# Moving operands of 256 tokens kept as two rows of 128, at another place in each partition

## The chip, the cores and the metric

The kernel runs on one core of a Trainium2 chip. The metric is the device time of one execution in microseconds; a lower time is better. The figure of a kernel is the median of several executions.

## What is computed

A transformer block and a second one of another build, for one sequence of 256 tokens of width 1024, in float32. The first block adds a gated sum of two mixers (a stick-breaking attention and an RWKV-7 time mix, eight heads of 64 each) and a SwiGLU network of width 2816. The second adds a mixer of a dilated-window attention and a short gated convolution, an attention to 256 tokens of a memory, and a network of width 4096 with a squared ReLU. Nearly all the work lies in products of the 256 tokens with weight matrices:

```python
proj = h @ w_in[l]
merged = (gates[..., :D] * (o_sb @ w_sb_out[l]) + gates[..., D:] * (o_rw @ w_rw_out[l]))
x = x + rms_norm(merged @ w_o[l], norm_mix_post[l])
h = rms_norm(x, norm_ffn_pre[l])
f = (jax.nn.silu(h @ w_ffn_gate[l]) * (h @ w_ffn_up[l])) @ w_ffn_down[l]
...
x = x + hybrid_mixer(rms_norm_2(x, g_mix), w_in, conv_w, g_attn_out, g_conv_out, w_out)
x = x + memory_cross_attention(rms_norm_2(x, g_xattn), rms_norm_2(mem, g_mem), w_q_mem, w_kv_mem, w_o_mem)
x = x + squared_relu_mlp(rms_norm_2(x, g_mlp), w_up, w_down)
return rms_norm_2(x, g_final)
```

## The kernel before, in words

Activations lie with features on the 128 partitions and tokens along them: a tile of `KC` chunks of 128 features holds, in each partition, `KC` times 256 tokens of 4 bytes. A float32 product is made of three products in the faster format `F32R`: each operand is kept as a rounded part (`xh`, `whi`) and a remainder (`xl`, `wlo`), and `whi` with `xh`, `whi` with `xl` and `wlo` with `xh` are summed in PSUM.

Weights come in slabs of 512 KB (`slab`, L185): one transfer on SyncE's queue, a copy on ScalarE that rounds (`whi`, L193), a subtraction on VectorE (`wlo`, L194). Three slabs are fetched ahead, in the order that `plan` wrote down at the start. For each slab `block` (L242) issues 24 matmuls at L258: two groups of 128 output features, four chunks of the contraction, three products each. A weight of 128 x 128 is the stationary operand, the 256 tokens of one chunk are the moving one. With `tok=True` it is the other way round: tokens are stationary, and 256 columns of the weight slab move; eight groups are made so (two for the values of the first attention, two for those of the dilated one, four for the values of the memory). The last product, `tokens` (L216), moves 512 columns of weights past tokens that are stationary (`ah`, `al`), through the helper `mm` (L273).

Where a tile lies in its partition is set by the order and the size of the pools; `shift` (L119) puts an unused tile of so many bytes ahead, and writes one element of it on GpSimd. So `PHASE` bytes stand before `xh`, and further shifts before the pools `one`, `gap` and `mlp`. With them every tile whose tokens move (`xh`, `xl`, `zh`, `zl`, `gh`, `gl`, `fh`, `fl`, `memh`, `meml`, `yh`, `yl`, `xoh`, `xol`, `sh`, `sl`, `oh`, `ol`) begins 192 bytes past a multiple of 512, a chunk is 1,024 bytes in one run, and slabs begin at a multiple of 512.

Tiles of tokens are written by `split` (L275: a copy on ScalarE, a subtraction on VectorE), by `normed` through it, and by `scaled` (L320: the same pair for one chunk, with a factor). In `hybrid` the factors of the norm lie in tiles of its own pool (`rm`, `r2`); the attention's factor is `ra`, the convolution's `rs`, both in the pool `tmp` with one buffer each. In `first`, chains of small steps (the recurrence, the first attention) are woven between the groups of matmuls, a step at each slab.

Matmuls whose operands are plain float32 (`px`, `py`, the transposes `tr`) take their columns at half the rate; in `px<-R,TT` the 128 moving columns are two runs of 64, in `px<-y,TT` one run. VectorE's product into `kap` (L596) works on runs of 64.

Of the kernel before, what the change touches and what calls it, by code (L numbers as in the profile page):

```python
# [8 lines left out]
F32 = mybir.dt.float32  # L9
F32R = mybir.dt.float32r  # L10
# [22 lines left out]
PHASE = 192  # L33
# [58 lines left out]

class Net:
    def __init__(self, ctx, tc, io):
        self.tc, self.nc, self.io = tc, tc.nc, io
        self.last_table = None
        self.queue, self.ready = [], []
        self.t2 = 3
        self.side = None
        nc = self.nc  # L100
        pool = lambda name, bufs=1, **k: ctx.enter_context(tc.tile_pool(name=name, bufs=bufs, **k))
        self.keep = pool("keep")
        self.cst = self.keep.tile([P, NRES], F32, name="cst")
        self.vec = self.keep.tile([P, NVEC], F32, name="vec")
        self.small = self.keep.tile([P, 8], F32, name="small")
        self.ones = self.keep.tile([P, P], F32, name="ones")
        self.pr = pool("wraw", 3)
        self.ph = pool("whi", 4)
        self.pl = pool("wlo", 4)


        acts = pool("acts")
        self.shift(acts, PHASE)
        self.xh = acts.tile([P, KC, T], F32R, name="xh")
        self.xl = acts.tile([P, KC, T], F32R, name="xl")
        self.zh = acts.tile([P, NP, T], F32R, name="zh")
        self.zl = acts.tile([P, NP, T], F32R, name="zl")
# [124 lines left out]
    def block(self, ps, name, g, b, xh, xl, tok):  # L242
        per = blocks(name)
        hi, lo, k0, m = self.next_slab(name, g * per + b)
        if isinstance(xh, list):
            xh, xl = xh[b], xl[b]
        cols = width(name) // P
        for c in range(cols):
            cc = slice(c * P, (c + 1) * P)
            for k in range(m):  # L250
                for t, (w, a) in enumerate(((hi, xh), (hi, xl), (lo, xh))):
                    first = b == 0 and c == 0 and k == 0 and t == 0
                    last = b == per - 1 and c == cols - 1 and k == m - 1 and t == 2
                    if tok:
                        lhsT, rhs = a[:, k0 + k, cc], w[:, k, :]
                    else:
                        lhsT, rhs = w[:, k, cc], a[:, k0 + k, :]
                    self.nc.tensor.matmul(ps[:, c, :], lhsT, rhs, start=first, stop=last,  # L258
                                          skip_group_check=True)
# [15 lines left out]
    def split(self, src, hi, lo):  # L275

        self.nc.scalar.copy(hi, src)
        self.nc.vector.tensor_sub(lo, src, hi.bitcast(F32))
# [14 lines left out]
    def rstd_sum(self, pool, parts, width, tag, square=None):  # L293
# [5 lines left out]
        r = pool.tile([P, T], F32, tag=tag, name=tag)  # L299
# [20 lines left out]
    def scaled(self, src, gname, hi, lo, first=0):  # L320

        for i, s in enumerate(src, first):
            for j in range(2):
                k, g = 2 * i + j, self.v(gname, 2 * i + j)
                self.nc.scalar.activation(hi[:, k, :], s[:, j, :], AF.Copy, scale=g)
                self.nc.vector.scalar_tensor_tensor(lo[:, k, :], s[:, j, :], g, hi[:, k, :].bitcast(F32),  # L326
# [17 lines left out]
    def normed(self, pool, src, r, gname, hi, lo):  # L344

        for i, s in enumerate(src):
# [4 lines left out]
            self.split(h, hi[:, 2 * i:2 * i + 2, :], lo[:, 2 * i:2 * i + 2, :])  # L351
# [75 lines left out]
def first(n):  # L427
    nc, tc = n.nc, n.tc
    with ExitStack() as ctx:
# [25 lines left out]
        gh = xg.tile([P, KC, T], F32R, name="gh")  # L455
        gl = xg.tile([P, KC, T], F32R, name="gl")
# [319 lines left out]
        sh = b4.tile([P, NP, T], F32R, tag="b4", name="sh")  # L776
        sl = b4.tile([P, NP, T], F32R, tag="b4", name="sl")
# [28 lines left out]
        def sb_values(j):  # L806
# [8 lines left out]
            n.split(of, sh[:, j, :], sl[:, j, :])  # L815
# [154 lines left out]
        def normalized():  # L970
# [4 lines left out]
            oh, ol = norm["o"] = [s4.tile([P, NP, T], F32R, tag="s4", name=k) for k in ("oh", "ol")]  # L975
# [12 lines left out]
            for i in range(2):  # L988
# [10 lines left out]
                n.split(yi, oh[:, ii, :], ol[:, ii, :])  # L999
# [14 lines left out]
        for g in range(4):  # L1014
# [6 lines left out]
            n.split(t, hi[:, 2 * g:2 * g + 2, :], lo[:, 2 * g:2 * g + 2, :])  # L1021
# [30 lines left out]
def ffn(n, tmp, wide, filler):  # L1052
    nc, tc = n.nc, n.tc
    with tc.tile_pool(name="ffn", bufs=1, reuse_waits="tile") as pool:
# [5 lines left out]
        fh = pool.tile([P, FF // P, T], F32R, name="fh")  # L1060
        fl = pool.tile([P, FF // P, T], F32R, name="fl")
        for g in range(FF // 256):
# [8 lines left out]
            n.split(m, fh[:, 2 * g:2 * g + 2, :], fl[:, 2 * g:2 * g + 2, :])  # L1071
# [4 lines left out]
def memory(n, mem, wide, tmp, kT, vm):  # L1076
# [4 lines left out]
    mh = mem.tile([P, KC, T], F32R, name="memh")  # L1081
    ml = mem.tile([P, KC, T], F32R, name="meml")
# [21 lines left out]
def hybrid(n, tmp, kv):  # L1104
    nc, tc = n.nc, n.tc
    with ExitStack() as ctx:
        pool = ctx.enter_context(tc.tile_pool(name="hyb", bufs=1, reuse_waits="tile"))
        yh = pool.tile([P, KC, T], F32R, name="yh")
        yl = pool.tile([P, KC, T], F32R, name="yl")
        r2 = pool.tile([P, T], F32, name="r2")  # L1110
        rs = []

        def norms():
            acc = n.squares(tmp, pairs(n.x))
            rs.append(pair(n.rstd_sum(pool, [acc], D, "rm", r2)))
# [90 lines left out]
        def conv_norm():  # L1206
            rc = n.rstd(tmp, pairs(cv), 512, "rs")
            kv(4, n.ax("kv").rearrange("p (c t) -> p c t", c=2))
            n.normed(tmp, pairs(cv), rc, "g_conv_out_2", yh[:, NP:, :], yl[:, NP:, :])
# [4 lines left out]
def cross(n, tmp, kT, vm, kv):  # L1214
    nc, tc = n.nc, n.tc
    with ExitStack() as ctx:
        pool = ctx.enter_context(tc.tile_pool(name="xat", bufs=1, reuse_waits="tile"))
        oh = pool.tile([P, KC, T], F32R, name="xoh")
        ol = pool.tile([P, KC, T], F32R, name="xol")
# [53 lines left out]
        def values(h):  # L1273
# [9 lines left out]
            nc.scalar.copy(oh[:, hh, :], po)  # L1283
            nc.vector.tensor_sub(ol[:, hh, :], po, oh[:, hh, :].bitcast(F32))
# [166 lines left out]
```

## Time and profile before

| | us |
|---|---|
| median of 3 runs | 845.67 (845.09 to 846.49) |
| the profiled execution | 845.12 |
| its span, first to last instruction | 843.4 |
| PE busy | 818.9 (97%) |
| VectorE busy | 565.0 (67%) |
| ScalarE busy | 464.5 (55%) |
| DMA, mean over the span | 169 GB/s |

A span runs from the first instruction of the program to the last; the execution's own time has a little around it. The chain is followed back from the last instruction, at each step to what released it. A matmul's duration in the trace is its latency: the next one starts before it ends, so PE reads as busy even where it starts matmuls more slowly than it could. How fast it goes is read from the starts in the timeline, or from a number of matmuls in a window.

### The profile page before, as it was taken

What the parts mean: (1) busy time and instruction counts of PE and PEld (TensorE: products, weight loads), DVE (VectorE), ACT (ScalarE), POOL (GpSimd) and SP (SyncE); (2) the same over time, 40 slices, a digit from 0 to 9 for tenths busy, and PEclk for the clock granted to TensorE, in tenths of its full rate; (3) what the DMA queues carried; (4) which work ended last, traced back from release to release, by engine and by line L of the source; (5) the groups of instructions that cost most, each with busy time, mean ns of one, the idle gap of its engine ahead of it and who ended that gap; (6) DMA issues with size and microseconds to landing.
All of it is one profiled execution on the core that took longest, in us unless ns stands there. A gap on an engine that the chain in (4) does not pass through costs nothing.

```text
span 843.4 us, 15763 instructions
## 1 busy us (share of the span) xinstructions
PE 818.9 (97%) x6508; PEld 777.1 (92%) x6508; DVE 565.0 (67%) x790; ACT 464.5 (55%) x714; POOL 5.7 (1%) x18
## 2 busy tenths in 40 slices
PE   5999998999999999999999999999999999999996
PEld 5898987999999999999999998999999999988884
DVE  6958689455978776666544876689676676654543
ACT  6587355643577654445444656457455575553432
POOL 0001001000000000000000000000000000000000
PEclk9999999999999999999999999999999999999998
DMA  8444433543464755555566464455534555555551
GB/s 289 141 150 152 141 127 119 163 148 99 136 245 147 228 189 185 194 181 191 167 192 184 155 209 146 147 180 193 179 100 155 194 177 178 198 188 186 194 181 51
DMA packets 44632, 142.88 MB, mean 169 GB/s; under 512 B 8977, under 2 KB 9745, under 8 KB 44305
## 3 DMA queue, kind: packets, MB, share of 16 engines
q1 hardware_dynamic: 43840, 139.25, 50.9%
q10 hardware_dynamic: 720, 2.63, 0.8%
q8 instruction: 51, 0.84, 0.4%
q14 instruction: 21, 0.16, 0.1%
HBM read 139.17 MB, written 2.69 MB: 168 GB/s over the span
## 4 chain that ended last, share of the span: by engine, by line
PE 81%; DVE 9%; ACT 4%; DMA 3%; issue 2%; DVEq 0%; ACTq 0%; SPq 0%
PE mm L258 59%; PE mm L273 11%; DVE wlo L194 3%; PE pz L273 2%; ACT whi L193 1%; DMA mraw<-in_mem 1%; PE rw L258 1%; PE po L273 1%; PE px L273 1%; PE mgnh L273 1%; PE ssum L273 1%; PE nv L273 1%; DVE prw L747 1%; PE kv L258 1%; DVE xl L326 1%
## 5 line engine op out<-in xcount | busy, mean ns | idle before, releaser
L194 DVE TENSOR_TENSOR wlo<-wraw,whi 128x1024 fp32r<-128x1024 f32 x254 | 308.2, 1215 | 191.0 <-ACT whi L193 190.2
L193 ACT CAST whi<-wraw 128x1024 fp32r<-128x1024 f32 x254 | 264.6, 1044 | 282.8 <-PE mm L258 162.5
L258 PE MATMUL mm<-xh,whi 128*128 128x256 f32 x1120 | 316.5, 283 | 0.0
L258 PE MATMUL mm<-xh,wlo 128*128 128x256 f32 x1120 | 313.4, 280 | 1.9 <-DVE wlo L194 1.9
L258 PE MATMUL mm<-xl,whi 128*128 128x256 f32 x1120 | 313.4, 280 | 0.0
L258 PEld LDWEIGHTS mm<-xh,wlo 128*128 128x128 f32 x1120 | 212.1, 189 | 3.2 <-DVE wlo L194 2.9
L258 PEld LDWEIGHTS mm<-xh,whi 128*128 128x128 f32 x1120 | 210.9, 188 | 3.7 <-issue 2.1
L258 PEld LDWEIGHTS mm<-xl,whi 128*128 128x128 f32 x1120 | 210.7, 188 | 0.9 <-issue 0.6
L273 PE MATMUL mm<-wlo,ah 128*128 128x512 f32 x128 | 50.6, 395 | 0.0
L273 PE MATMUL mm<-whi,al 128*128 128x512 f32 x128 | 50.6, 395 | 0.0
L273 PE MATMUL mm<-whi,ah 128*128 128x512 f32 x128 | 50.6, 395 | 0.0
L258 PE MATMUL mm<-fh,whi 128*128 128x256 f32 x176 | 49.5, 281 | 0.0
L258 PE MATMUL mm<-fl,whi 128*128 128x256 f32 x176 | 49.5, 281 | 0.0
L258 PE MATMUL mm<-fh,wlo 128*128 128x256 f32 x176 | 49.5, 281 | 0.0
L258 PEld LDWEIGHTS mm<-fh,wlo 128*128 128x128 f32 x176 | 33.8, 192 | 0.0
L258 PEld LDWEIGHTS mm<-fh,whi 128*128 128x128 f32 x176 | 33.0, 188 | 0.0
L258 PEld LDWEIGHTS mm<-fl,whi 128*128 128x128 f32 x176 | 33.0, 188 | 0.0
L273 PEld LDWEIGHTS mm<-whi,al 128*128 128x128 f32 x128 | 24.1, 188 | 5.8
L273 PEld LDWEIGHTS mm<-wlo,ah 128*128 128x128 f32 x128 | 24.1, 188 | 5.8
L273 PEld LDWEIGHTS mm<-whi,ah 128*128 128x128 f32 x128 | 24.1, 188 | 5.7
L258 PE MATMUL rw<-gh,whi 128*128 128x256 f32 x48 | 14.9, 310 | 8.6 <-ACT whi L193 8.6
L258 PE MATMUL mm<-memh,whi 128*128 128x256 f32 x64 | 18.5, 288 | 0.0
(352 smaller groups left out, 1377.4 us busy)
## 6 DMA issues: line engine op xcount, KB each, us to landing
wraw<-in_w_up SPq DMA_DIRECT2D x32, 512.0 KB, 3.3
wraw<-in_w_down SPq DMA_DIRECT2D x32, 512.0 KB, 3.3
wraw<-in_w_in SPq DMA_DIRECT2D x24, 512.0 KB, 4.1
wraw<-in_w_ffn_gate SPq DMA_DIRECT2D x22, 512.0 KB, 3.4
wraw<-in_w_ffn_up SPq DMA_DIRECT2D x22, 512.0 KB, 3.3
wraw<-in_w_ffn_down SPq DMA_DIRECT2D x20, 512.0 KB, 3.6
wraw<-in_w_gate SPq DMA_DIRECT2D x16, 512.0 KB, 3.3
wraw<-in_w_kv_mem SPq DMA_DIRECT2D x16, 512.0 KB, 3.3
```

What stands on the lines that cost most here:

```text
L193: nc.scalar.copy(hi[:, :w], raw[:, :w])
L194: nc.vector.tensor_sub(lo[:, :w], raw[:, :w], hi[:, :w].bitcast(F32))
L258: self.nc.tensor.matmul(ps[:, c, :], lhsT, rhs, start=first, stop=last, skip_group_check=True)
L273: self.nc.tensor.matmul(out, lhsT, rhs, start=start, stop=stop, skip_group_check=True)
L326: self.nc.vector.scalar_tensor_tensor(lo[:, k, :], s[:, j, :], g, hi[:, k, :].bitcast(F32), op0=ALU.mult, op1=ALU.subtract)
L747: nc.vector.tensor_mul(pr, left[:, r:r + 4, :].rearrange("p r (o i) -> p r o i", o=1).to_broadcast([P, 4, 16, 16]), right.rearrange("p (o ...
```

## The change

The 256 tokens of a chunk are kept as two halves of 128 in two rows of the tile (`halved`). A row holds all chunks' halves, 512 bytes each, and is padded so that it is an odd multiple of 256 bytes long. So the first half of every chunk begins 128 bytes past a multiple of 512 (`PHASE` is 128 now), the second half 384, and a moving operand is two runs of 128 tokens. `in_two` gives the same view of a tile that stays in one run, of a PSUM bank and of a source. `sh`, `sl`, `oh` and `ol` stay in one run, and begin at 416 and 32 past a multiple of 512. The shifts change; the factors of `memory` and `hybrid` take other buffers, of which those in `tmp` are shared with `ra` and `rs`. `ah` and `al`, stationary in the last stage, begin 192 past a multiple of 512, 320 before. No instruction is added or moved on any engine, other than one memset of a shift less on GpSimd. The same line in `fh`'s form stands for `memh`, `xoh` and their remainders; the callers that write `hi[:, 2 * i:2 * i + 2, :]` drop the last index.

```diff
-PHASE = 192
+PHASE = 128
...
+def halved(pool, chunks, name):
+    w = chunks * P
+    w += (64 - w) % 128
+    t = pool.tile([P, 2, w], F32R, name=name)
+    return t[:, :, :chunks * P].rearrange("p h (k s) -> p k h s", s=P)
+
+def in_two(t):
+    return t.rearrange("p (h s) -> p h s", h=2) if len(t.shape) == 2 else t.rearrange("p k (h s) -> p k h s", h=2)
...
         acts = pool("acts")
         self.shift(acts, PHASE)
-        self.xh = acts.tile([P, KC, T], F32R, name="xh")
-        self.xl = acts.tile([P, KC, T], F32R, name="xl")
-        self.zh = acts.tile([P, NP, T], F32R, name="zh")
-        self.zl = acts.tile([P, NP, T], F32R, name="zl")
+        self.xh, self.xl = (halved(acts, KC, k) for k in ("xh", "xl"))
+        self.zh, self.zl = (halved(acts, NP, k) for k in ("zh", "zl"))
...
                     if tok:
-                        lhsT, rhs = a[:, k0 + k, cc], w[:, k, :]
+                        o, lhsT, rhs = ps[:, c, :], a[:, k0 + k, c], w[:, k, :]
                     else:
-                        lhsT, rhs = w[:, k, cc], a[:, k0 + k, :]
-                    self.nc.tensor.matmul(ps[:, c, :], lhsT, rhs, start=first, stop=last,
-                                          skip_group_check=True)
+                        o, lhsT, rhs = in_two(ps[:, c, :]), w[:, k, cc], a[:, k0 + k]
+                    self.nc.tensor.matmul(o, lhsT, rhs, start=first, stop=last, skip_group_check=True)
...
     def split(self, src, hi, lo):
 
+        if len(hi.shape) > len(src.shape):
+            src = in_two(src)
         self.nc.scalar.copy(hi, src)
         self.nc.vector.tensor_sub(lo, src, hi.bitcast(F32))
...
-                self.nc.scalar.activation(hi[:, k, :], s[:, j, :], AF.Copy, scale=g)
-                self.nc.vector.scalar_tensor_tensor(lo[:, k, :], s[:, j, :], g, hi[:, k, :].bitcast(F32),
+                t = in_two(s[:, j, :])
+                self.nc.scalar.activation(hi[:, k], t, AF.Copy, scale=g)
+                self.nc.vector.scalar_tensor_tensor(lo[:, k], t, g, hi[:, k].bitcast(F32),
                                                     op0=ALU.mult, op1=ALU.subtract)
...
         one = ctx.enter_context(tc.tile_pool(name="one", bufs=1))
-        n.shift(one, 608)
         s4 = ctx.enter_context(tc.tile_pool(name="s4", bufs=14))
         dr = ctx.enter_context(tc.tile_pool(name="dr", bufs=1, space=DRAM))
-        n.shift(ctx.enter_context(tc.tile_pool(name="gap", bufs=1)), 640)
...
-        gh = xg.tile([P, KC, T], F32R, name="gh")
-        gl = xg.tile([P, KC, T], F32R, name="gl")
+        n.shift(xg, 224)
+        gh, gl = (halved(xg, KC, k) for k in ("gh", "gl"))
...
-        sh = b4.tile([P, NP, T], F32R, tag="b4", name="sh")
-        sl = b4.tile([P, NP, T], F32R, tag="b4", name="sl")
+        sh, sl = (in_two(b4.tile([P, NP, T], F32R, tag="b4", name=k)) for k in ("sh", "sl"))
...
-        fh = pool.tile([P, FF // P, T], F32R, name="fh")
-        fl = pool.tile([P, FF // P, T], F32R, name="fl")
+        fh, fl = (halved(pool, FF // P, k) for k in ("fh", "fl"))
...
-    r = pair(n.rstd_sum(mem, [acc], D, "rk"))
+    rk = mem.tile([P, T], F32, name="rk")
+    r = pair(n.rstd_sum(tmp, [acc], D, None, out=rk))
...
-        yh = pool.tile([P, KC, T], F32R, name="yh")
-        yl = pool.tile([P, KC, T], F32R, name="yl")
-        r2 = pool.tile([P, T], F32, name="r2")
+        yh, yl = (halved(pool, KC, k) for k in ("yh", "yl"))
+        r2 = tmp.tile([P, T], F32, tag="rs", name="r2")
...
-            rs.append(pair(n.rstd_sum(pool, [acc], D, "rm", r2)))
+            rs.append(pair(n.rstd_sum(tmp, [acc], D, "ra", r2)))
...
-            nc.scalar.copy(oh[:, hh, :], po)
-            nc.vector.tensor_sub(ol[:, hh, :], po, oh[:, hh, :].bitcast(F32))
+            n.split(po, oh[:, hh], ol[:, hh])
...
-        n.shift(pool, 832 - PHASE)
+        n.shift(pool, 64)
```

## Rows read from the trace of the kernel before

**Rows 1.** The page, part 1: busy time, share, instructions of each engine.

```profile
PE 818.9 (97%) x6508; PEld 777.1 (92%) x6508; DVE 565.0 (67%) x790; ACT 464.5 (55%) x714; POOL 5.7 (1%) x18
```

**Rows 2.** The page, part 4: shares by line of the chain that ended last.

```profile
PE mm L258 59%; PE mm L273 11%; DVE wlo L194 3%; PE pz L273 2%; ACT whi L193 1%; DMA mraw<-in_mem 1%; PE rw L258 1%; PE po L273 1%; PE px L273 1%; PE mgnh L273 1%; PE ssum L273 1%; PE nv L273 1%; DVE prw L747 1%; PE kv L258 1%; DVE xl L326 1%
```

**Rows 3.** Windows of line L258: stretch, length us, PE busy (matmuls), clock, DMA, GB/s.

```profile
0.00:843.40 843.40, 637.57 (x5280) 1.00 0.52 169
...
31.00:250.00 219.00, 150.46 (x1198) 1.00 0.45 146
```

**Rows 4.** The waits: engine, line, waited for, us in total, times, longest.

```profile
ACT whi L193 <- PE mm L258: 162.5, 116, 4.7
```

**Rows 5.** Timeline of PE at 300 us: start us, us, engine, line, out<-in.

```profile
300.07 0.28 PE L258 MATMUL mm<-xl,whi 128*128 128x256 f32 x1
...
317.03 0.28 PE L258 MATMUL mm<-xl,whi 128*128 128x256 f32 x1
```

**Rows 6.** Timeline of PE at 700 us.

```profile
700.08 0.28 PE L258 MATMUL mm<-xh,whi 128*128 128x256 f32 x1
...
716.40 0.28 PE L258 MATMUL mm<-xh,whi 128*128 128x256 f32 x1
```

**Rows 7.** Windows, ten slower stretches: length, PE, PEld, DVE, ACT, POOL busy, clock.

```profile
288.80:463.90 175.10, 175.10 (x1489) 175.10 (x1488) 105.28 (x111) 84.89 (x99) 0.00 (x0) 1.00 0.59 187
...
sum 313.70, PE 313.70 PEld 313.70 DVE 216.66 ACT 167.76 POOL 0.00; mean PE 31.37 PEld 31.37 DVE 21.67 ACT 16.78 POOL 0.00
```

**Rows 8.** Windows, seven quicker stretches.

```profile
694.90:745.90 51.00, 51.00 (x453) 51.00 (x452) 33.88 (x38) 28.92 (x38) 0.00 (x0) 1.00 0.58 194
sum 117.00, PE 117.00 PEld 117.00 DVE 86.32 ACT 68.63 POOL 0.00; mean PE 16.71 PEld 16.71 DVE 12.33 ACT 9.80 POOL 0.00
```

**Rows 9.** Timeline of PE: four transposes in a row.

```profile
64.90 0.60 PE L616 MATMUL tr<-cst,AR 128*128 128x128 f32 x4
```

**Rows 10.** Timeline of PE: matmuls of 128 columns at half rate, sixteen each.

```profile
169.48 1.95 PE L273 MATMUL px<-y,TT 128*128 128x128 f32 x16
171.26 1.95 PE L273 MATMUL px<-R,TT 128*128 128x128 f32 x16
```

**Rows 11.** Timeline of PE in the last stage, 512 columns each.

```profile
760.21 0.39 PE L273 MATMUL mm<-wlo,ah 128*128 128x512 f32 x1
...
793.81 0.39 PE L273 MATMUL mm<-wlo,ah 128*128 128x512 f32 x1
```

**Rows 12.** The page, parts 5 and 6: a slab's subtraction; a slab's transfer.

```profile
L194 DVE TENSOR_TENSOR wlo<-wraw,whi 128x1024 fp32r<-128x1024 f32 x254 | 308.2, 1215 | 191.0 <-ACT whi L193 190.2
...
wraw<-in_w_up SPq DMA_DIRECT2D x32, 512.0 KB, 3.3
```

**Rows 13.** Groups of VectorE's instructions: xcount | busy us, mean ns | idle before.

```profile
L278 DVE TENSOR_TENSOR fl<-m,fh 128x512 fp32r<-128x512 f32 x11 | 7.5, 685 | 0.0
...
L596 DVE TENSOR_TENSOR kap<-a,EN 128x512 f32<-128x512 f32 x2 | 1.3, 684 | 0.0
```

**Rows 14.** Timelines of VectorE and ScalarE: last readers and next writers of two buffers.

```profile
531.46 0.69 DVE L1189 TENSOR_TENSOR bg<-mm,rm 128x512 f32<-128x512 f32 x1 [0.52 <-PE mm L258]
...
545.18 0.69 DVE L1192 TENSOR_TENSOR cg<-mm,r 128x512 f32<-128x512 f32 x1 [0.60 <-PE mm L258]
...
546.56 0.42 ACT L156 ACTIVATE ra<-lg 128x256 f32<-128x256 f32 x1
...
569.60 0.42 ACT L156 ACTIVATE rs<-lg 128x256 f32<-128x256 f32 x1
```

**Rows 15.** Timeline of PE: matmuls that move the weights, slower, then quicker.

```profile
109.40 0.28 PE L258 MATMUL mm<-whi,xh 128*128 128x256 f32 x1
...
113.64 0.28 PE L258 MATMUL mm<-whi,xh 128*128 128x256 f32 x1
...
609.53 0.28 PE L258 MATMUL mm<-whi,meml 128*128 128x256 f32 x1
...
612.93 0.28 PE L258 MATMUL mm<-whi,meml 128*128 128x256 f32 x1
```

More of the change, by code (lines that the diff above doesn't have):

```diff
@@ L291, in sumsq, with rstd_sum @@
         return a2
-    def rstd_sum(self, pool, parts, width, tag, square=None):
+    def rstd_sum(self, pool, parts, width, tag, square=None, out=None):
         ps = self.ax("ssum")
@@ L298, in rstd_sum @@
         lg = pool.tile([P, T], F32, tag="t1", name="lg", bufs=1)
-        r = pool.tile([P, T], F32, tag=tag, name=tag)
+        r = pool.tile([P, T], F32, tag=tag, name=tag) if out is None else out
         self.act(lg, ps[:, :T], AF.Ln, bias=self.eps, scale=1.0 / width)
@@ L350, in normed @@
                     h[:, j, :], s[:, j, :], self.v(gname, 2 * i + j), r, op0=ALU.mult, op1=ALU.mult)
-            self.split(h, hi[:, 2 * i:2 * i + 2, :], lo[:, 2 * i:2 * i + 2, :])
+            self.split(h, hi[:, 2 * i:2 * i + 2], lo[:, 2 * i:2 * i + 2])
 def staggered(count, *stages, apart=1):
@@ L814, in sb_values @@
             nc.vector.tensor_copy(of, po[:, :T])
-            n.split(of, sh[:, j, :], sl[:, j, :])
+            n.split(of, sh[:, j], sl[:, j])
         early.close()
@@ L974, in normalized @@
             nc.sync.dma_start(flat(gb), park[1])
-            oh, ol = norm["o"] = [s4.tile([P, NP, T], F32R, tag="s4", name=k) for k in ("oh", "ol")]
+            oh, ol = norm["o"] = [in_two(s4.tile([P, NP, T], F32R, tag="s4", name=k)) for k in ("oh", "ol")]
             pv = {}
@@ L998, in normalized @@
                 nc.vector.tensor_add(yi, yi, gb[:, ii, :])
-                n.split(yi, oh[:, ii, :], ol[:, ii, :])
+                n.split(yi, oh[:, ii], ol[:, ii])
             yield
@@ L1020, in first @@
             hi, lo = (n.zh, n.zl) if g < 2 else (n.xh, n.xl)
-            n.split(t, hi[:, 2 * g:2 * g + 2, :], lo[:, 2 * g:2 * g + 2, :])
+            n.split(t, hi[:, 2 * g:2 * g + 2], lo[:, 2 * g:2 * g + 2])
 def branch_add(n, tmp, pool, w, hi, lo, gname, filler, after, side=False):
@@ L1070, in ffn @@
             nc.vector.tensor_mul(m, m, s)
-            n.split(m, fh[:, 2 * g:2 * g + 2, :], fl[:, 2 * g:2 * g + 2, :])
+            n.split(m, fh[:, 2 * g:2 * g + 2], fl[:, 2 * g:2 * g + 2])
         n.table("natural_log_exp_and_others")
@@ L1080, in memory @@
     nc.scalar.dma_start(m.rearrange("p c t -> p (c t)"), n.io["mem"])
-    mh = mem.tile([P, KC, T], F32R, name="memh")
-    ml = mem.tile([P, KC, T], F32R, name="meml")
+    mh, ml = (halved(mem, KC, k) for k in ("memh", "meml"))
     n.scaled(pairs(m), "g_mem_2", mh, ml)
     acc = n.squares(tmp, pairs(m))
-    r = pair(n.rstd_sum(mem, [acc], D, "rk"))
+    rk = mem.tile([P, T], F32, name="rk")
+    r = pair(n.rstd_sum(tmp, [acc], D, None, out=rk))
     rt = n.rstd_tok(mem, [acc], D, out=n.small[:, 4:6])
@@ L1208, in conv_norm @@
             kv(4, n.ax("kv").rearrange("p (c t) -> p c t", c=2))
-            n.normed(tmp, pairs(cv), rc, "g_conv_out_2", yh[:, NP:, :], yl[:, NP:, :])
+            n.normed(tmp, pairs(cv), rc, "g_conv_out_2", yh[:, NP:], yl[:, NP:])
         plain_add(n, "w_out_2", yh, yl, conv_norm)
@@ L1217, in cross @@
         pool = ctx.enter_context(tc.tile_pool(name="xat", bufs=1, reuse_waits="tile"))
-        oh = pool.tile([P, KC, T], F32R, name="xoh")
-        ol = pool.tile([P, KC, T], F32R, name="xol")
+        oh, ol = (halved(pool, KC, k) for k in ("xoh", "xol"))
         n.scaled(pairs(n.x), "g_xattn_2", n.xh, n.xl)
```

## The prediction

> **What bounds the kernel now.** I read the page first, then the chain, then the timeline of TensorE by the starts of its matmuls. The page has PE busy for 97% of the 843.4 us, and VectorE for 67%, ScalarE for 55% [rows 1]; of the chain that ended last 59% is one line, the matmul of `block` (L258) [rows 2]. That line issues 5,280 of the matmuls [rows 3]. What feeds it waits for it: ScalarE's copy of a slab sits idle 162.5 us in all until PE has done with a buffer [rows 4]. So what counts is how far apart PE starts its matmuls, which the page doesn't show: the 281 ns of a matmul are its latency, and several are under way at once. The starts tell. From 300.07 to 317.03 us there are 144 steps from one matmul to the next, 117.8 ns each [rows 5]; from 700.08 to 716.40 us there are as many, 113.3 ns each, by the same line on tiles of the same layout [rows 6]. Both levels last for hundreds of matmuls and change only where the stream is broken. 256 columns at 2.4 GHz, the clock that these stretches show as granted (1.00 [rows 7, 8]), are 106.7 ns. So each matmul carries 11.1 or 6.7 ns above its columns.
>
> How many run at which level: ten stretches of the slower level sum to 313.7 us, 2,663 matmuls, the longest of them 175.1 us [rows 7]; seven of the quicker one sum to 117.0 us, 1,032 matmuls [rows 8]. The other 1,585 stand in short runs and at waits; I looked at a few and count 700 at each level and 185 as set by waits. That makes 3,363 slower and 1,732 quicker ones.
>
> What the 11.1 and 6.7 ns are: floors come from other matmuls. Four transposes in a row take 0.60 us, of which the last alone is some 0.27, so they start 110 ns apart, 3 ns over the same 106.7 [rows 9]. So 2 to 3 ns belong to any matmul. Sixteen of 128 columns at half the rate start (1.95 - 0.28)/15 = 111 to 112 ns apart [rows 10]. That leaves about 4.4 ns in the quicker level and 8.9 in the slower: one stall or two of 4.4 ns. The 512-column matmuls of the last stage start 233.3 ns apart (144 steps from 760.21 to 793.81 us [rows 11]), 20.0 over their columns, so 17.6, four such stalls. Two in 1,024 bytes of moving operand, four in 2,048: the slower level reads as **one stall for each 512 bytes of the moving operand**, and the quicker one hides every second. That is a reading of three numbers, not something that a row says.
>
> **The change part by part.** The order of instructions is the same on every engine, and the sizes are too; only addresses and access patterns differ, besides one memset less on the idle POOL. Three things to price.
>
> Moving operands. Before, every moving tile begins 192 bytes past a multiple of 512 and is read in one run, so each piece of 512 bytes starts where the last one did, modulo 512. Now one half starts at 128, the other at 384, the next matmul at 128 again: each piece starts 256 off from the last. Of the 5,280 matmuls, 384 are not touched, for they move the weights (`tok`: eight groups of 48), nor 192 that read `sh`, `sl`, `oh` and `ol`, still in one run; 4,704 are, 89%. What a matmul with two full-rate runs costs stands in no row. From below: the transposes' 110 ns or the columns with 2.3 ns, 109. From above: a second run could cost one more stall, 117.8 + 4.4 = 122.2 ns. The nearest row on the runs themselves is half rate: `px<-R,TT` moves two runs of 64 and takes 1.95 us for sixteen, as `px<-y,TT` does with one run [rows 10]; a second run costs nothing there. I take 111.7, the nearest of the levels that show no stall. Then 0.89 x 3,363 x 6.1 ns = 18.3 us and 0.89 x 1,732 x 1.66 ns = 2.6 us, together 20.9 us.
>
> Not all of it arrives. From 31 to 250 us only 1,198 of the line's matmuls stand in 219 us [rows 3]; between them run chains of small steps on VectorE and ScalarE that get no shorter. That is 23% of the matmuls and 4.7 us of the gain; I let half of it be lost, 2.4 us. Elsewhere what feeds PE has room: a slab of 24 matmuls lasts 2.7 to 2.8 us, VectorE needs 1.2 us of it for the slab, and the slab's transfer lands 3.3 us after its issue, with three slabs fetched ahead [rows 12].
>
> What writes the tiles. 27 pairs of a 512-column copy and subtraction, and the pairs of 256 columns in `scaled`, now write two runs per chunk. VectorE's product into `kap`, in runs of 64, takes 684 ns for 512 columns, the subtraction into `fl` in one run 685 [rows 13]: price 0 at both ends.
>
> Buffers shared. In `hybrid` the factor of L1124 now lies in the buffer that the attention's factor `ra` takes next, and the other one in the buffer of `rs`. Their last readers start at 531.46 and 545.18 us and take 0.69 us; the next writers come at 546.56 and 569.60 us [rows 14]. 14 and 23 us of cover, so 0; without it a write would wait less than the 0.69 us. In the last stage only the stationary tile moves (from 320 to 192 past a multiple of 512): 0, with 1.7 us to either side (a stall of 4.4 ns more or less for each of its 384 matmuls).
>
> Sum: 20.9 - 2.4 = 18.5 us. The profiled execution took 845.1 us in all (1.7 more than its span), so 826.6; it is 0.5 below the median of the three runs, so **827 us**.
>
> A page of the Trainium skill speaks of the floor: "TensorE: Matmul & The Clock Gate", section "Back-to-back issue gap", gives a lone matmul's spacing as its columns at 2.4 GHz plus 2.5 ns, which would be 109.2 ns here. The rows that run line L258 don't agree (113.3 and 117.8 ns); if the new layout met the formula, the sum would be 816 us.
>
> **Rivals.** (a) *One stall stays*: all matmuls go to the quicker level, which the trace shows for up to 51 us at a time [rows 8]. 0.89 x 3,363 x 4.45 ns = 13.3 us, less 1.5 in the first third: 834 us.
>
> (b) *Where the operand lies plays no part*, and the two levels are states into which the stream falls after a break. For it: both levels occur at one and the same address, and matmuls that move the weights, at 0 past a multiple of 512, show 117.8 ns (36 steps from 109.40 to 113.64 us) and 113.3 ns (30 steps from 609.53 to 612.93 us) as well [rows 15]. Then the change does nothing that it says, and only the mixture is drawn anew: between 834 (all quicker) and 853 (all slower, 0.89 x 1,732 x 4.45 = 6.9 us), most likely near 846. "SBUF — State Buffer", section "Who interferes with whom", of the Trainium skill says as much: moving operand and weight load have read ports of their own, and "PE and ACT never wait on anyone". That 4.4 and 8.9 ns are there at all shows that something is waited for, but not that it lies in the layout.
>
> (c) *Slower: the second run costs a stall of its own.* The generator of addresses has to leave the row after 128 columns; at half rate that hides [rows 10], at full rate it needn't. It decides as soon as a run's start costs more than the stalls that the offset saves. If it pins everything to the slower level, 853 us; if it adds one stall to each touched matmul, 4,704 x 4.45 ns = 20.9 us, 867 us.
>
> **How the numbers follow.** Forecast (no stall left, 109 to 111.7 ns) 0.42; (a) 0.20; (b) 0.18; (c) 0.20, of which 0.08 at 853 and 0.12 at 867. I put most on the layout mattering because the stalls scale with the moving bytes and not with weight loads: the 512-column stage has one weight load per matmul too, but twice the stalls. What a measurement here can tell from no change is about 0.2%, 1.7 us. The forecast and (a) are faster by more, 0.62; of (b) 0.05 falls there by a luckier mixture, 0.09 within, 0.04 slower; (c) is slower. So 0.67, 0.09 and 0.24. The range reaches down to 814 us (all touched matmuls at 109 ns, 0.89 x (3,363 x 8.8 + 1,732 x 4.4 ns) = 33 us, less 3.8 and rounded out) and up to 853, which takes in (a), (b) and the milder half of (c).
>
> **What would show it.** Right: the starts of L258's successor stand 109 to 112 ns apart in long stretches, at one level throughout; the slab's copies on ScalarE come closer together; the 512-column stage stays at 233 ns. (a): 113.3 ns everywhere. (b): both old levels, in other places. (c): 117.8 or 122 ns. Wrong altogether: waits that PE didn't have before, or a subtraction into a halved tile that takes much more than 685 ns.

## The result and the profile after

The changed kernel takes 851.07 us (median of 4, 850.62 to 851.23) where the kernel before takes 845.57 beside it (845.09 to 846.49): 1.0069 times as long, 95% interval 1.0056 to 1.0082. It is slower by 0.7%, some 5.5 us, and the interval lies wholly above 1; 827 was forecast.

| us | before | after |
|---|---|---|
| span of the profiled execution | 843.4 | 849.3 |
| 5,280 matmuls of the line of `block` (L258, now L269), from each start to PE's next | 634.9 | 643.2 |
| 383 of 512 columns in the last stage, the same | 89.4 | 87.7 |
| PE's other steps | 102.6 | 101.7 |

The last three rows add up the steps between PE's starts in the two traces, waits included, so that their sum follows the span (5.7 of 5.9 us) is no finding. The finding is where it stands: in the line of `block`, 8.3 us more, while the other two rows fell by 2.6. Within that line the unbroken steps (those under 126 ns, 5,153 and 5,156 of them) grew from 599.2 to 612.1 us, 12.9 more, and the some 125 longer ones, which hold the waits, shrank from 35.6 to 31.1. The page of the changed kernel, parts 1 and 4, and the wait that answers to [rows 4]:

```profile
PE 828.5 (98%) x6508; PEld 789.3 (93%) x6508; DVE 565.4 (67%) x790; ACT 465.0 (55%) x714; POOL 5.6 (1%) x17
...
PE mm L269 65%; PE mm L283 11%; DVE wlo L205 2%; PE pz L283 2%; DMA wraw<-in_w_rw 1%; PE rw L269 1%; PE px L283 1%; PE po L283 1%; PE mgnh L283 1%; ACT whi L204 1%; PE ssum L283 1%; PE nv L283 1%; DVE prw L758 1%; PE kv L269 1%; DVE xl L339 1%
```

```profile
ACT whi L204 <- PE mm L269: 164.4, 113, 4.7
```

VectorE and ScalarE work as long as before [rows 1], ScalarE waits for PE about as long as before, and the line's share of the chain goes from 59% [rows 2] to 65%. That is more than 8.3 us can make of 849.3 (1%), so the chain also runs through this line at times when it ran elsewhere before; the added time itself is read from the steps. Where it lies, the windows show: the stretch that held 1,489 matmuls in 175.10 us [rows 7], and the one that held 453 in 51.00 us [rows 8], in the changed kernel (length, then PE, PEld, DVE, ACT, POOL busy, then the granted clock):

```profile
288.70:465.20 176.50, 176.50 (x1489) 176.47 (x1488) 105.41 (x112) 85.26 (x99) 0.00 (x0) 1.00 0.58 186
...
700.00:753.60 53.60, 53.60 (x454) 53.60 (x453) 34.11 (x38) 28.99 (x38) 0.00 (x0) 1.00 0.55 185
```

The two old levels, 117.8 and 113.3 ns, have become one in these two stretches, 118.5 and 118.1 by these windows, whose edges cut a matmul; from first start to last the runs of 1,486 and of 454 steps come to 118.67 and 118.66 ns. The clock is 1.00 in both. The timeline of PE shows that it is a new level and not a mixture of the old ones (start us, us, engine, line, out<-in):

```profile
300.10 0.28 PE L269 MATMUL mm<-xh,wlo 128*128 128x256 f32 x1
300.21 0.28 PE L269 MATMUL mm<-xh,whi 128*128 128x256 f32 x1
300.33 0.28 PE L269 MATMUL mm<-xl,whi 128*128 128x256 f32 x1
300.45 0.28 PE L269 MATMUL mm<-xh,wlo 128*128 128x256 f32 x1
300.57 0.28 PE L269 MATMUL mm<-xh,whi 128*128 128x256 f32 x1
300.69 0.28 PE L269 MATMUL mm<-xl,whi 128*128 128x256 f32 x1
...
317.18 0.28 PE L269 MATMUL mm<-xh,wlo 128*128 128x256 f32 x1
```

From 300.10 to 317.18 us there are again 144 steps, now of 118.6 ns, against 117.8 in [rows 5]. In the nanoseconds of the trace the steps read 115, 118, 122, 120, 119 and again, a pattern of five that the kernel before doesn't have. Two more places moved though their operands are still in one run: the last stage, and the matmuls that move the weights.

```profile
765.13 0.39 PE L283 MATMUL mm<-whi,al 128*128 128x512 f32 x1
...
798.09 0.39 PE L283 MATMUL mm<-whi,al 128*128 128x512 f32 x1
```

```profile
108.89 0.28 PE L269 MATMUL mm<-whi,xl 128*128 128x256 f32 x1
...
114.34 0.28 PE L269 MATMUL mm<-wlo,xh 128*128 128x256 f32 x1
```

144 steps of 512 columns take 32.96 us, 228.9 ns each, against 233.3 in [rows 11]; 46 steps that move the weights take 118.5 ns, where [rows 15] showed 117.8 and 113.3. In both the moving operand stands where it stood, and only the stationary one lies elsewhere. So a theory of the moving operand alone cannot be whole.

### The profile page after: what moved, and what is told of

It is laid out like the page before. It is cut to its first block, busy times and chain, and to the rows that moved or that the text cites. A ratio compares the mean times of both kernels' runs of the same rounds, so it can differ in the third digit from the quotient of the medians.

```text
span 849.3 us, 15766 instructions
## 1 busy us (share of the span) xinstructions
PE 828.5 (98%) x6508; PEld 789.3 (93%) x6508; DVE 565.4 (67%) x790; ACT 465.0 (55%) x714; POOL 5.6 (1%) x17
## 4 chain that ended last, share of the span: by engine, by line
PE 87%; DVE 8%; DMA 2%; ACT 2%; issue 1%; SPq 0%; ACTq 0%; DVEq 0%
PE mm L269 65%; PE mm L283 11%; DVE wlo L205 2%; PE pz L283 2%; DMA wraw<-in_w_rw 1%; PE rw L269 1%; PE px L283 1%; PE po L283 1%; PE mgnh L283 1%; ACT whi L204 1%; PE ssum L283 1%; PE nv L283 1%; DVE prw L758 1%; PE kv L269 1%; DVE xl L339 1%
## 5 line engine op out<-in xcount | busy, mean ns | idle before, releaser
L269 PE MATMUL mm<-xh,whi 128*128 128x256 f32 x1120 | 319.3, 285 | 0.0
L269 PE MATMUL mm<-xh,wlo 128*128 128x256 f32 x1120 | 316.3, 282 | 0.7 <-DVE wlo L205 0.6
L269 PE MATMUL mm<-xl,whi 128*128 128x256 f32 x1120 | 316.3, 282 | 0.0
L269 PEld LDWEIGHTS mm<-xh,whi 128*128 128x128 f32 x1120 | 211.1, 188 | 3.7 <-issue 2.1
L269 PEld LDWEIGHTS mm<-xh,wlo 128*128 128x128 f32 x1120 | 211.0, 188 | 1.8 <-DVE wlo L205 1.1
L269 PEld LDWEIGHTS mm<-xl,whi 128*128 128x128 f32 x1120 | 211.1, 188 | 0.9 <-issue 0.6
L269 PE MATMUL mm<-fh,whi 128*128 128x256 f32 x176 | 49.5, 281 | 0.0
L269 PE MATMUL mm<-fh,wlo 128*128 128x256 f32 x176 | 49.5, 281 | 0.0
L269 PE MATMUL mm<-fl,whi 128*128 128x256 f32 x176 | 49.5, 281 | 0.0
L269 PEld LDWEIGHTS mm<-fh,whi 128*128 128x128 f32 x176 | 33.1, 188 | 0.0
L269 PEld LDWEIGHTS mm<-fh,wlo 128*128 128x128 f32 x176 | 33.1, 188 | 0.0
L269 PEld LDWEIGHTS mm<-fl,whi 128*128 128x128 f32 x176 | 33.1, 188 | 0.0
L269 PE MATMUL rw<-gh,whi 128*128 128x256 f32 x48 | 15.0, 312 | 8.8 <-ACT whi L204 8.8
L269 PE MATMUL mm<-memh,whi 128*128 128x256 f32 x64 | 18.8, 293 | 0.0
```

The costliest lines, as they stand in the source:

```text
L269: self.nc.tensor.matmul(o, lhsT, rhs, start=first, stop=last, skip_group_check=True)
```

## The experiments

Each ratio below is to the kernel before, run beside it on the same chip (843.8 to 844.2 us there, 845.6 beside the changed kernel), so ratios are compared and not times. Three theories went into the runs. **Place**: what counts is where the moving operand lies against the weights. **Second run**: each additional run of a moving operand costs something of its own. **State**: places play no part, the start of a stream decides.

### 1. A map without the network, quiet and busy

TensorE alone streams 72 matmuls at a time in the order of `block`. Each layout is tried twice, after one and after five matmuls of 64 columns. The core of it, where m is the place of the moving operand, d the distance of its second run, and ws the place of the weights:

```diff
+    lhsT = w[:, s * 2048 + ws // 4:][:, k * 256 + c * P:][:, :P]
+    if kind == ONE:
+        rhs = xs[a][:, (k0 + k) * T:][:, :T]
+    else:
+        row = 1024 + d // 4
+        rhs = xs[a][:, :2 * row].rearrange("p (h s) -> p h s", h=2)[:, :, (k0 + k) * P:(k0 + k + 1) * P]
```

> This kernel leaves out the whole network. TensorE alone streams matmuls of 128x256 float32r in the order of block (hi, hi, lo weights for each piece of 128 rows), 72 at a time, for 47 layouts, each twice: the moving operand in one run at 12 places modulo 512 bytes, in two runs whose places differ by 256 at 11 places, in two runs at one and the same place at 6, in two runs at six other distances, four places of the weights, and 512 columns with eight places of the weights. ScalarE and VectorE rest. Place theory: the spacing hangs on where moving operand and weights lie to each other; one run at 192 gives 113.3 or 117.8 ns, two runs at 128 and 384 give 118.7 or 120 ns, other places give other levels, some as low as 113.3; 512 columns give 228.9 ns at 192 and 233.3 at 320. Second-run theory: every layout in one run gives 113.3 or 117.8 ns wherever it lies, and every layout in two runs 118.7 or 120, also where both runs lie at one place. State theory: no layout has a level of its own, and the two turns of one layout differ as much as two layouts do.

The timeline of PE in the quiet run, by streams (start us, length us). A stream of 72 behind small matmuls has a first step of 0.20 us, then 70 steps, and the last one's 0.28 us; the very first comes behind others of its size and has 71 equal steps.

```profile
38.34 8.32 PE L48 MATMUL ps<-x,w 128*128 128x256 f32 x72
...
46.53 8.41 PE L48 MATMUL ps<-x,w 128*128 128x256 f32 x72
...
55.25 8.79 PE L48 MATMUL ps<-x,w 128*128 128x256 f32 x72
...
73.00 8.87 PE L48 MATMUL ps<-x,w 128*128 128x256 f32 x72
...
250.47 8.78 PE L48 MATMUL ps<-x,w 128*128 128x256 f32 x72
...
259.12 8.88 PE L48 MATMUL ps<-x,w 128*128 128x256 f32 x72
...
339.38 8.42 PE L48 MATMUL ps<-x,w 128*128 128x256 f32 x72
...
444.86 8.73 PE L48 MATMUL ps<-x,w 128*128 128x256 f32 x72
...
658.25 8.79 PE L48 MATMUL ps<-x,w 128*128 128x256 f32 x72
...
693.63 8.87 PE L48 MATMUL ps<-x,w 128*128 128x256 f32 x72
...
746.49 8.64 PE L32 MATMUL ps<-w,x 128*128 128x512 f32 x36
...
772.26 8.43 PE L32 MATMUL ps<-w,x 128*128 128x512 f32 x36
```

In order: one run at 192, twice ((8.41 - 0.48)/70 = 113.3 ns); one run at 128 (118.7); one run at 0 (120.0); two runs at 128 and 384, twice (118.6 and 120.0); two runs at 192 and 448 (113.4); two runs, both at 192 (117.8); one run at 192 with the weights at 64 (118.7), and with the weights at 192 too (119.9 by the row, 120.0 once settled); 512 columns with the stationary at 320 (233.3) and at 0 (226.7). By the distance, with the steps worked out from the starts in the trace:

| moving against weights, modulo 256 bytes | one run, ns | two runs, 256 apart, ns |
|---|---|---|
| 0 | 120.0 | 120.0 |
| 32 | 116.7, 117.8 | 116.7, 117.8 |
| 64 | 117.8 | 117.8 |
| 96 | 120.0 | 120.0 |
| 128 | 118.7, 120.0 | 118.7, 120.0 |
| 192 | 113.3, 117.8 | 113.3, 117.8 |
| 224 | 118.4 | 118.3 |

The two columns are the same. A second run costs nothing, a distance of 256 between the runs buys nothing, and the place of the moving operand against the weights says which levels there are. A second run counts by its place alone: 64, 128 or 192 bytes further on than a first one at 128, it gives 120.0, 118.5 and 117.8 ns. On the weights' side, moving them by 64 does the same as moving the operand back by 64. The same map doesn't hold for 512 columns, which run at 226.7 ns at a distance of 0, where 256 columns show their 120.0. The second-run theory falls, and of the state theory only this is left: at some distances the start picks between two levels.

The map also has the levels of both kernels. Before, the moving operands stood at 192 (113.3 or 117.8) and the last stage's stationary tile at 320 (233.3). After, they stand at 128 (118.7 or 120.0) and at 192 (228.9), and the matmuls that move the weights went from a distance of 64 (117.8) to 128 (118.7). One is missing: the 113.3 ns of [rows 15], which no start gave at a distance of 64 with hi and lo weights at one place. Why the kernel reaches it there stays open.

> The same kernel without the network, with ScalarE copying and VectorE subtracting 1,024 columns without a pause beside it (on other buffers). If the stalls come from the other engines' reads and writes, the levels rise here against the quiet run by several ns; if they are between TensorE's own two reads (place theory) or in the second run itself, each layout keeps its level to within 0.5 ns.

Its page, part 1, and the streams at 192 and at 0 in its timeline:

```profile
PE 854.1 (75%) x6674; PEld 829.4 (73%) x6674; DVE 1103.5 (97%) x901; ACT 958.2 (84%) x908; POOL 0.3 (0%) x5
```

```profile
46.20 8.41 PE L48 MATMUL ps<-x,w 128*128 128x256 f32 x72
...
72.68 8.87 PE L48 MATMUL ps<-x,w 128*128 128x256 f32 x72
```

8.41 and 8.87 us as in the quiet run; no layout moved by more than 0.1 ns. ScalarE and VectorE, working on other buffers, take nothing from PE's matmuls here. Nor are the levels the DMA's doing: it moved 3 GB/s in either map and 186 beside the 1,489 matmuls of the changed kernel, and both show 118.7 ns at 128. The Trainium skill, "SBUF — State Buffer", section "Who interferes with whom", states that PE and ACT never wait on anyone, which agrees with this run as far as other engines go. But the same section's table gives PE one read port for the moving operand and an independent one for the weight load. If that is read as saying that where the one operand lies cannot matter to the other, the map's rows contradict it: up to 6.7 ns of 120.

### 2. One part of the change at a time, in the whole kernel

The changed kernel with one run instead of two, at the same places:

```diff
-    t = pool.tile([P, 2, w], F32R, name=name)
-    return t[:, :, :chunks * P].rearrange("p h (k s) -> p k h s", s=P)
+    t = pool.tile([P, 2 * w], F32R, name=name)
+    return t[:, :chunks * T].rearrange("p (k h s) -> p k h s", h=2, s=P)
```

> The change with its moving tiles in one run of 256 tokens again, at the same places (128 past a multiple of 512), and everything else as changed. Place theory: as slow as the change, 851 us within 1.5, levels 118.7 and 120 ns. Second-run theory (the second run costs a stall of its own): back at 845 or below, 113.3 and 117.8 ns; only the last stage's 228.9 ns stays.

852.55 us, 1.0105 times the kernel before (1.0077 to 1.0134). The halves are gone and the loss is not.

The changed kernel with its two halves, begun elsewhere:

```diff
-PHASE = 128
+PHASE = 192
```

> The change with the halves kept, but its first offset 192 instead of 128, so that they lie at 192 and 448 past a multiple of 512, and the last stage's stationary tile at 256. Place theory: the two old levels come back, 113.3 and 117.8 ns, and the last stage goes to 226.7 ns (from 233.3 before, 2.5 us for 383 matmuls): 843 us, between 834 and 850 by how the two levels mix. Second-run theory: 118.7 to 122 ns as with the change, 850 to 853 us.

841.00 us, 0.9971 times (0.9956 to 0.9987). The halves are there and the loss is gone. The same 1,489 matmuls, in the windows of the run with one run at 128 and then of that with the halves at 192 and 448:

```profile
290.70:467.20 176.50, 176.50 (x1489) 176.50 (x1488) 105.24 (x111) 84.95 (x99) 0.00 (x0) 1.00 0.55 184
```

```profile
287.70:462.80 175.10, 175.10 (x1489) 175.10 (x1488) 105.34 (x111) 85.06 (x99) 0.00 (x0) 1.00 0.56 186
```

176.50 is the changed kernel's time, 175.10 that of the kernel before [rows 7], to the last digit. With the halves at 192 the short stretch falls back too: 454 steps at 113.37 ns, as before. Over all the steps that the change touches the mean is 116.30 ns with two runs at 192 and 448 and 116.33 with one run at 192 (4,572 and 4,558 unbroken steps). What made this run faster than the kernel before is mostly the last stage: its stationary tile lies at 256 here, and its 383 steps sum to 86.8 us instead of 89.4, as in the next run.

The kernel before, with the last stage's stationary tile alone moved:

```diff
-        n.shift(pool, 832 - PHASE)
+        n.shift(pool, 1024 - PHASE)
```

> The kernel before, with the stationary tile of the last stage alone moved from 320 to 0 past a multiple of 512. Place theory: 226.7 ns for each of 383 matmuls of 512 columns instead of 233.3, 2.5 us less, 843.0 us. Second-run and state theories: nothing changes there, 845.6 us.

841.99 us, 0.9974 times (0.9959 to 0.9988). The timeline of PE in the last stage:

```profile
760.09 0.39 PE L273 MATMUL mm<-whi,ah 128*128 128x512 f32 x1
...
792.73 0.39 PE L273 MATMUL mm<-whi,ah 128*128 128x512 f32 x1
```

144 steps of 226.7 ns, 2.5 us less for the 383; the ratio gives 2.2 us of 843.8. Nothing moving was touched here.

### 3. Finer places, and what the start decides

> A second map without the network, six starts of each layout after six kinds of break (one or more small matmuls, or an idle wait for ScalarE). In the first map the level followed the place of the moving operand against the weights modulo 256 bytes, and only a distance of 192 reached 113.3 ns, sometimes 117.8. Place theory: fine steps about 192 show how wide the good place is (113.3 within some 16 bytes, 116 to 120 ns beyond); two runs at 192 and 320 read as a mixture of the levels of 192 and 64, 115 to 118 ns; the start decides between 113.3 and 117.8 ns at 192. 512 columns show 226.7 ns with the stationary at 0 or near, against 233.3 before. State theory's rest (the levels of a place differ only by the start): then the kind of break, the same at every layout, should sort them.

Three starts each of one run at 192, of two runs at 192 and 448, and of one run at 192 with the lo weights 128 bytes off the hi ones modulo 256, from the timeline. A stream of 36 has 34 steps besides its first, and where the third start begins that one is 0.17 us:

```profile
38.64 4.33 PE L56 MATMUL ps<-x,w 128*128 128x256 f32 x36
...
43.28 4.49 PE L56 MATMUL ps<-x,w 128*128 128x256 f32 x36
...
47.66 4.46 PE L56 MATMUL ps<-x,w 128*128 128x256 f32 x36
...
631.87 4.35 PE L56 MATMUL ps<-x,w 128*128 128x256 f32 x36
...
636.53 4.49 PE L56 MATMUL ps<-x,w 128*128 128x256 f32 x36
...
640.91 4.46 PE L56 MATMUL ps<-x,w 128*128 128x256 f32 x36
...
941.23 4.38 PE L56 MATMUL ps<-x,w 128*128 128x256 f32 x36
...
945.92 4.34 PE L56 MATMUL ps<-x,w 128*128 128x256 f32 x36
...
950.15 4.31 PE L56 MATMUL ps<-x,w 128*128 128x256 f32 x36
```

At 192 four of six starts settle at 113.3 ns and two stay at 117.8, and they are the same two for one run, for two runs 256 apart and for two runs at one place. So the two levels of the kernel before are two states of one layout, and what goes ahead of the stream picks one. The kind of break alone doesn't fix which. In the quiet map two runs at 192 and 448 and two runs both at 192 each began behind five small matmuls, at 339.38 and 444.86 us, and went to 113.4 and 117.8 ns; and in the fourth map below the same six breaks as here leave 117.8 ns behind the first, second and fifth, not behind the second and third. With the lo weights 128 off, all six end at 113.3 ns, after 3 to 14 matmuls; so do all six with the second group of weight columns 128 off, and none with the lo weights 64 or 192 off. Four guesses of the expectation missed. The good place is not 16 bytes wide (8 bytes to either side of 192 give 119.7 to 120.8 ns, 4 bytes above it 119.9 to 122.2). 112 reaches 113.3 as well, after 7 to 11 matmuls. Two runs at 192 and 320 give 118.0 to 118.2, just above the 115 to 118 guessed. And near 0 the 512 columns keep 226.7 ns only in part: with the stationary 16 bytes to either side one start of six and three of six show it, 32 bytes off none does.

> A third map without the network, six starts of each layout after the same six kinds of break. The second map had all six starts at 192 end at 113.3 ns once the lo weights lay 128 bytes past the hi ones modulo 256, after 2 to 15 matmuls, while with both at one place two of six stayed at 117.8. Place theory: the same here at 192; other places of the moving operand stay at 116 to 120 ns; tok's streams (weights move) at a distance of 64 from the stationary show 117.8 with both weights at one place, and may find 113.3 with the lo weights 128 apart; for 512 columns with lo 128 apart some place of the stationary still reaches 226.7 to 229 ns. State theory: the mixture of 113.3 and 117.8 by the start stays in every row.

At 192 all six starts reach 113.3 again. At 64 three of six did, where I had expected none. The streams that move the weights stay at 117.8 at the distance that the kernel uses, with the lo weights apart or not; at a distance of 192 with both weights at one place they show 113.3 in five of six. For 512 columns with the lo weights apart the best stationary place is 128 (228.9 ns), and 0 gives 231 to 233.

### 4. What the maps point to, in the whole kernel

```diff
         self.ph = pool("whi", 4)
+        self.shift(pool("apart"), 128)
         self.pl = pool("wlo", 4)
...
-        self.shift(acts, PHASE)
+        self.shift(acts, PHASE - 128)
```

> The kernel before with one change: the buffers of the lo weights begin 128 bytes past a multiple of 512 instead of 0 (a gap of 128 bytes ahead of them, 128 bytes less of shift behind). Place theory, as the second map has it: nearly all matmuls of the line at 113.3 ns; 3,363 x 4.45 ns = 15.0 us, less half of the 23% that stand in the first third, 13 us: 831 us, between 828 and 835; the last stage keeps 233 ns or changes by up to 2.5 us either way. State theory (the start alone decides, the mixture is drawn anew): 834 to 850. If only the moving operand's own place counts: 844 us, nothing changes.

832.23 us, 0.9864 times (0.9837 to 0.9892): 11.5 us faster than the kernel before, by 128 bytes of address and no instruction more than one memset. The same 1,489 matmuls, and part 1 of its page:

```profile
284.40:453.00 168.60, 168.60 (x1489) 168.60 (x1488) 105.34 (x112) 85.47 (x99) 0.00 (x0) 1.00 0.58 193
```

```profile
PE 805.0 (97%) x6508; PEld 764.7 (92%) x6508; DVE 564.2 (68%) x790; ACT 464.8 (56%) x714; POOL 5.7 (1%) x19
```

168.60 us instead of 175.10, 113.3 ns from end to end. Of the unbroken steps of the line some 4,400 stand at 113.3 (some 1,750 before), counted by the mean of neighbouring steps. By the two traces the sum of the line's steps falls from 634.9 to 621.0 us, 13.9 less, of which 10.4 in the unbroken ones; the expectation had 15.0, and 13 after its deduction for the first third.

With the last stage's stationary at 0 as well (`832 - PHASE` to `1024 - PHASE`):

> The same with the stationary tile of the last stage at 0 past a multiple of 512 as well. Place theory: 1 to 2.5 us below the run before it (226.7 ns for the two thirds that move hi weights, 227 to 233 for the third that moves lo ones), 829 us, between 826 and 834. State theory: as the run before.

832.32 us, 0.9855 times (0.9836 to 0.9875), no gain over the run before: the last stage stood at 233.3 ns, so 0 is a good place only as long as hi and lo weights share one. The expectation, which took two thirds of the matmuls as free of it, missed. With the place that the third map gave (`896 - PHASE`, 384):

> The kernel before with the lo weights 128 past a multiple of 512 and the last stage's stationary tile at 384 instead of 320. The third map gives 228.8 ns there (231.1 in the run with the lo weights alone moved), 383 x 2.3 ns = 0.9 us less than that run's 832.2: 831.3 us, between 829 and 833. The theory that only the start decides: 834 to 850.

831.54 us, 0.9847 times (0.9827 to 0.9867), the fastest of this study; 228.9 ns in the last stage. Against the run with the lo weights alone it is less than the two intervals can tell apart.

And the change's halves in that layout, at 192 and 448:

> The change's two halves, begun at 192 and 448, with the lo weights at 128 past a multiple of 512 and the last stage's stationary tile at 384. If a second run costs nothing of itself: as the run with one run of 256 tokens, 831 to 833 us, where two small pairs of tiles left at 96 and 480 cost up to 1 us more; most of the line at 113.3 ns. If the second run costs a stall once the others are gone: 117.8 to 120 ns, 845 us or more.

833.35 us, 0.9866 times (0.9844 to 0.9889), and its window of the 1,489:

```profile
288.60:457.20 168.60, 168.60 (x1489) 168.60 (x1488) 105.40 (x112) 85.49 (x99) 0.00 (x0) 1.00 0.60 194
```

168.60 us again. Also at the lowest level a second run costs nothing. The time is a little over the 831 to 833 us expected; of the 1.8 us to the run before, 0.9 stand in the steps of `sh`, `sl`, `oh` and `ol`, the small pairs left at 96 and 480 (23.9 us for 23.1).

### 5. Weight columns, moving columns, bf16

> A fourth map without the network, again six starts of each layout: float32r with 128, 64 and 32 columns of weights beside 256 moving columns, 384 and 512 moving columns, and bf16 (weights of 256 bytes a row, 512 moving columns are 1,024 bytes), each at distances of 0, 64, 128 and 192 (bf16 with 256 columns in steps of 32). If the stall is between the reading of the next weights and of the moving operand (place theory), fewer weight columns leave it shorter or gone: with 32 columns every place comes near 113.3 ns, and the spread between places shrinks with the columns. If the moving operand alone pays for its place, 64 and 32 weight columns show the same 113.3 to 120 ns by place as 128. bf16: its rows are half as long, so stalls of half the size or none, 107 to 113 ns at 256 columns.

First starts from the timeline: 128 weight columns at a distance of 0, 64 columns at 0, 32 columns at 64 and at 192, and bf16 at 0:

```profile
37.58 4.55 PE L35 MATMUL ps<-x,w 128*128 128x256 f32 x36
...
150.13 4.29 PE L35 MATMUL ps<-x,w 128*64 128x256 f32 x36
...
287.25 4.37 PE L35 MATMUL ps<-x,w 128*32 128x256 f32 x36
...
341.35 4.25 PE L35 MATMUL ps<-x,w 128*32 128x256 f32 x36
...
564.40 4.10 PE L35 MATMUL ps<-xb,wb 128*128 128x256 bf16 x36
```

By the starts: at a distance of 0, 120.0 ns with 128 weight columns, 113.3 with 64 (and 116.6 to 119.2 at most starts of the other distances). With 32 columns, 113.3 at all starts at 192 and at four of six at 128, but 116.6 to 116.8 at four of six at 64 and 117.8 at three of six at 0. So the expectation held in part only: the spread between places is 113.3 to 120.0 ns with 128 and with 64 columns and 113.3 to 117.8 with 32, and at 192 five of six starts are slower with 64 columns (118.8 to 119.2 ns) than all six with 128 there (113.3 or 117.8). That the weights are a party to it fits, for only their width changed, and with it the rows of the output; the first map shows it without that, where the weights alone were moved. bf16 shows one level at every distance and start: 109.2 ns at 256 columns and 215.8 at 512.

## Why the prediction was wrong

**The bound: right.** PE's spacing is what counts: the unbroken steps of the line grew by 12.9 us and nothing else on PE grew, and in the run with the lo weights moved 13.9 us less in the line's steps went with a profiled span that was 14.6 us shorter (843.4 to 828.8; 11.5 by the runs beside each other). The count of 3,363 and 1,732 matmuls on the two levels holds too (some 3,300 and 1,750 by the mean of neighbouring steps). That the levels change only where the stream is broken is nearly so: at 234 us of the trace before, the unbroken steps go from 113 to 118 ns six matmuls after the moving tile has changed from `oh` to `zh`. And the deduction for waits was a term of the right kind: of the 12.9 us, 4.6 came back as shorter waits.

**The step that failed** is the price of the touched matmuls, "I take 111.7, the nearest of the levels that show no stall", and under it the reading "one stall for each 512 bytes of the moving operand", taken from three numbers. In none of the layouts tried does a float32r stream settle below 113.3 ns for 256 columns or 226.7 for 512; 113.3 is the lowest level that anything reached, with 128, 64 and 32 weight columns alike, and no run shows a stall in it that a layout could take away. The transposes [rows 9] and the half-rate matmuls [rows 10] were not of the same kind and gave a floor that doesn't exist here. And what sits on top of that level is not counted per 512 bytes of the moving operand; it hangs on the distance of that operand from the weights. The 18.3 us from the slower level and the 2.6 from the quicker were both to come from halves lying 256 apart. The levels repeat every 256 bytes, so a half that lies 256 further on lies at the same place as far as they go: two runs at 192 and 448 repeat the levels of one run at 192. What the change did move is the base, from 192 to 128, and there streams settle at 118.7 or 120.0 ns. The touched steps, where unbroken, went from 116.33 to 118.78 ns; with the waits between them that is 9.7 us more over 4,645 steps.

**Two runs at full rate cost nothing: right**, and so [rows 10] was read rightly there. Rival (c) came near the time (853) by luck, with a mechanism that the runs refute.

**The untouched matmuls** I had left at their levels. They moved, since their places did: the 384 that move the weights by +0.3 us, the 192 on `sh`, `sl`, `oh` and `ol` by +0.4. The last stage, priced "0, with 1.7 us to either side", gained those 1.7 us: its stationary tile went from a poor place to a better one.

**Writers and buffers: right at 0.** The subtraction into the halved `fl` in the groups of VectorE (xcount, busy us, mean ns):

```profile
L290 DVE TENSOR_TENSOR fl<-m,fh 128x512 fp32r<-128x512 f32 x11 | 7.5, 685 | 0.0
```

685 ns, as in [rows 13]. The buffers shared in `hybrid` [rows 14] keep their cover: their next writers start at 549.2 and 572.4 us, 14.7 and 23.9 after the last readers end.

**What the evidence could not tell apart.** [rows 15] showed both levels with the weights moving at 0, at another place than all other moving tiles. I used it for rival (b) alone. It fits the forecast's reading too, for there as well each piece of 512 bytes began where the last one did, so it decided nothing between the two; and the stalls per 512 bytes were a reading of three numbers from streams that differed in more than the place. No row varied the place of one operand alone, which is what the maps then did. Rival (b) was right in its first half (two states of one layout) and wrong in its second (places play no part).

## What to carry to other kernels

A level of spacing that holds for hundreds of matmuls and changes at a break can be a state of one layout. Before pricing a change that moves addresses, vary one operand's address at a time in a stream of matmuls alone: both operands count, by their distance. A map of 47 layouts took one run and refuted the plan, and a second one named the place (lo weights 128 bytes off) that gave 11.5 us, where the change as planned lost 5.5. A floor is taken from the same data type and rate, not from other matmuls.

## What the runs showed of the hardware

- In the layouts tried, float32r at 128 x 256 keeps 113.3 ns at best and 226.7 for 512 columns, twice that, so 6.25% over its columns at the granted clock of 1.00; 384 columns keep 173.3 at best, 8.3% over theirs. The Trainium skill, "TensorE: Matmul & The Clock Gate", section "Back-to-back issue gap", gives columns at 2.4 GHz plus 2.5 ns for an isolated matmul, 109.2 and 215.8 ns: streams of bf16 show these here, float32r does not.
- The spacing of float32r depends on the moving operand's distance from the weights: 113.3 to 120.0 ns in steps of 32 bytes, and 4 bytes above the good place cost 6.5 ns or more. The levels repeat with a distance of 256 bytes; bf16 shows none of it.
- At a distance of 192 a stream settles at 113.3 or at 117.8 ns by what went ahead of it, and can keep that for as long as it lasts (175.1 us in this kernel). With hi and lo weights 128 bytes apart all twelve starts tried found 113.3 by themselves.

Open, and not tried: where on the way from the memory to TensorE the two operands meet, what of a stream's start picks its state, and why a stream with its weights apart leaves the slower state while one with both at one place does not.
